# Attention's weight-value products in four visits a pair of heads instead of nine

## The chip, the cores and the metric

The kernel runs on one core of one Trainium2 chip. A core has a matrix engine (TensorE, in the profile PE for matmuls and PEld for the loading of their stationary operand), three engines for elementwise work (VectorE = DVE, ScalarE = ACT, GpSimd = POOL) and a queue that mostly issues DMAs (SyncE = SP). The metric is the device time of one launch in microseconds; lower is better.

## The reference

A decoder trunk with one state-space layer and one attention layer, each followed by a gated convolutional feed-forward block. 1024 tokens and 16 learned meta tokens give 1040 positions of width 1024. The change lies in the attention: 16 heads of width 64, causal without the diagonal, with "stick-breaking" weights in place of a softmax. Cut to what matters:

```python
logits = einsum('bthd,bshd->bhts', q[:, t0:t1], k[:, :t1]) * 64 ** -0.5
visible = s_idx < t_idx
log_keep = where(visible, log_sigmoid(-logits), 0.0)
later = cumsum(log_keep, axis=3, reverse=True) - log_keep
w = exp(where(visible, log_sigmoid(logits) + later, -inf))
out = einsum('bhts,bshd->bthd', w, v[:, :t1])
```

The kernel computes the sum of logarithms as a running product: with keep = sigmoid(-logit) and beta = sigmoid(logit), the weight of key s is beta(s) times the product of keep over all later visible keys.

## The kernel before

The stage before the attention leaves the normalised stream in 16 large SBUF tiles (8 high parts, 8 low parts). The heads are worked off in 8 pairs; the two heads of a pair (index `a`) use the partitions 0 to 63 and 64 to 127. The positions are cut into 9 chunks `i` of 116 (`CB`; the last has 112), and three chunks make a token tile `jj` of 348.

A pair has 18 steps, `steps = [(i, jj) for i in range(9) for jj in range(i // 3, -1, -1)]`: for every chunk of queries the token tiles of keys from its own one back to the first. The loop `for p in range(PAIRS): for n, (i, jj) in enumerate(steps)` does in every step, in this order:

- `weigh(i, jj)`: for either head two matmuls for the logits (L1642, tile `lg`, two PSUM banks), two sigmoids on ScalarE (L1645 `kp` = keep, L1646 `bt` = beta), on the diagonal a mask on GpSimd (L1651), a scan on VectorE for the running product (L1655; a chunk's later tiles begin from the value of the one before) and a multiplication (L1656). `kp` has 6 buffers, `bt` 8.
- `place()`: transposes of projected values (L1606, tile `pv`) and their scaling into `v` on VectorE (L1608).
- half a projection (`half`, matmuls L200 to L202, tile `pj`): 24 matmuls in two steps make a token tile of keys, queries or values; the dictionary `halves` gives each of the 18 steps one half, in steps 0 to 7 for this pair and in 8 to 17 for the next one (keys 0 in steps 8 and 9, queries 0 in 10 and 11, queries 1 in 12 and 13, keys 1 in 14 and 15, values 0 in 16 and 17). `pj` has two PSUM banks, used in turn. A query projection is emptied one step after its second half by `stack` (L1589 on ScalarE, then L1593 on VectorE, tile `qs`), which is put behind that step's scans.
- `chores`: one piece of the preparation of the next pair's weights (L1543 on ScalarE, L1544 on VectorE, tile `wl`).
- `flush(LAG)`: first `values` for a chunk whose weights are complete, then `turn` for the step three before this one.

`turn` transposes the weights of both heads, one block of 116 keys at a time (L1669, tile `wT`, three PSUM banks that `pv` shares), and copies them to SBUF on ScalarE (L1673, tile `wt`). `values` multiplies them with `v` (L1683): for each block `c` of keys two products, one for each head, into the partitions 0 to 63 and 64 to 127 of one PSUM bank `po` (a single buffer); ScalarE copies `po` to `o` (L1684), and at the end of a token tile its queue stores `o` to DRAM (L1686). Those products are in plain float32 and show in the profile as two records each. I call one call of `values` a visit.

`wt` takes its tiles from the pool `Q` of 28 large buffers, in which the stream, the keys, and the queries of token tiles 1 and 2 lie too. SP's queue carries the weight loads and the moves of keys and queries between partitions; the change touches none of them.

In the attention stage PE, DVE, ACT and POOL keep the order of the program (`manual_schedule`); outside of it the scheduler chooses. After the last step, `while turns or ready: flush(0)` empties what is left, and the output projection follows.

Of the kernel before, what the change touches and what calls it, by code (L numbers as in the profile page):

```python
# [10 lines left out]
AF = mybir.ActivationFunctionType  # L11
# [9 lines left out]
CB = 116  # L21
CH = [(c * CB, min(CB, L - c * CB)) for c in range(9)]
TT = [(0, 348), (348, 348), (696, 344)]
TW = 352
QW = 1056
# [37 lines left out]
NPOOL = 3  # L63
DT0 = 0
LAG = 2

NW = 8
SUMS = ((6, 1), (3, 6), (7, 6), (3, 5), (5, 7)), ((4, 7), (2, 1))
# [35 lines left out]
class Trunk:  # L104
# [1085 lines left out]
    def up(self, layer, w0, forms, rest, pool):  # L1190
# [8 lines left out]
        def block(b, t, w, late=None):  # L1199
# [32 lines left out]
            u2 = copy(y)  # L1232
            yield
            z = product(3, (self.ex if next(turn) else self.lg)("p"))
            p5 = copy(z)
            add(z, z, u2)
# [420 lines left out]
            prev[a] = kp  # L1657
        return [bt for _, bt, _ in out]

    def turn(self, i, jj, bt, wt):  # L1660

        nc = self.nc
        nt = CH[i][1]
        blocks = range(3 * jj, min(3 * jj + 3, i + 1))
        for a in range(2):
            pt = self.sm("wT")
            for x, c in enumerate(blocks):
                ns = CH[c][1]
                nc.tensor.transpose(pt[:ns, x * CB : x * CB + nt], bt[a][:nt, x * CB : x * CB + ns], self.ident[:nt, :nt])  # L1669
            spans = [(0, len(blocks), CB)] if CH[blocks[-1]][1] == CB else [(0, 2, CB), (2, 3, CH[8][1])]  # L1670
            for x, y, ns in spans:
                src = pt[:ns, : 3 * CB].rearrange("p (c t) -> p c t", t=CB)[:, x:y, :nt]
                nc.scalar.activation(wt[a][:ns, 3 * jj + x : 3 * jj + y, :nt], src, AF.Copy)  # L1673

    def values(self, p, i, wt, v, o, od):

        nc = self.nc
        t0, nt = CH[i]
        j, c0 = i // 3, (i % 3) * CB
        po = self.ex("po")  # L1680
        for x, c in enumerate(c for jj in range(j, -1, -1) for c in range(3 * jj, min(3 * jj + 3, i + 1))):
            for a in range(2):
                nc.tensor.matmul(po[64 * a : 64 * a + 64, :nt], v[: CH[c][1], c, 64 * a : 64 * a + 64], wt[a][: CH[c][1], c, :nt], start=x == 0, stop=x == i)  # L1683
        nc.scalar.activation(o[:, c0 : c0 + nt], po[:, :nt], AF.Copy)  # L1684
        if i % 3 == 2:
            nc.scalar.dma_start(od[p, :, TT[j][0] : t0 + nt], o[:, : TT[j][1]])  # L1686

    def attention(self, u, pool):


        od = self.dp.tile([PAIRS, P, L], F32, tag="o_d", name="o_d")
        steps = [(i, jj) for i in range(9) for jj in range(i // 3, -1, -1)]

        halves = {(own, n0 + h): (kind, j, h) for own, n0, kind, j in (
            (0, 0, "v", 1), (0, 2, "q", 2), (0, 4, "k", 2), (0, 6, "v", 2),
            (-1, 8, "k", 0), (-1, 10, "q", 0), (-1, 12, "q", 1), (-1, 14, "k", 1), (-1, 16, "v", 0)) for h in range(2)}
        loads = {(-1, 4): "k", (-1, 7): "q", (-1, 9): "v"}
        pairs = [self.heads(u, p, pool) for p in range(PAIRS)]
        turns, ready, wts, os, late, chores = [], [], {}, {}, [], []

        def flush(n):
            while ready:
                p, i = ready.pop()
                if i % 3 == 0:
                    os[p] = self.tmp("o")
                self.values(p, i, wts.pop((p, i)), pairs[p].v, os[p], od)
            if len(turns) > n:
                p, i, jj, bt = turns.pop(0)
                if jj == i // 3:
                    wts[p, i] = [self.Q("wt")[:, : 9 * CB].rearrange("p (c t) -> p c t", t=CB) for _ in range(2)]  # L1710
                self.turn(i, jj, bt, wts[p, i])
                if jj == 0:
                    ready.append((p, i))

        first = pairs[0]
        for kind in "kqv":
            for f in first.load(kind):
                f()
        for kind, j, bank in (("k", 0, self.mm), ("q", 0, self.mm), ("k", 1, self.sm), ("q", 1, self.ex)):
            for h in range(2):  # L1720
                for f in first.half(kind, j, h, bank):
                    f()
            if (kind, j) == ("k", 0):
                self.late_factors()
        self.token_factors(u[KD], pool)
        for p in range(PAIRS):
            prev = None
            for n, (i, jj) in enumerate(steps):
                if jj == i // 3:
                    prev = [None, None]  # L1730
                now = {0: pairs[p], -1: pairs[p + 1]} if p + 1 < PAIRS else {0: pairs[p]}
                bt = self.weigh(i, jj, now[0].qd[i // 3], now[0].ks, prev, pool)
                todo, late = late, []
                now[0].place()
                if p == 0 and n < 2:
                    first.half("v", 0, n)
                for own, pair in now.items():
                    if (own, n) in halves:
                        late += pair.half(*halves[own, n])
                for f in todo + chores[:1]:  # L1740
                    f()
                del chores[:1]
                for own, pair in now.items():
                    if (own, n) in loads:
                        chores += pair.load(loads[own, n])
                flush(LAG)
                turns.append((p, i, jj, bt))
        while turns or ready:
            flush(0)
        return od  # L1750
# [204 lines left out]
```

## Time and profile before

| | |
|---|---|
| Runs before, median of 3 | 2870.42 us (2870.36 to 2876.0) |
| Profiled execution, span from first to last instruction | 2866.2 us; no other time is recorded of it |
| Attention stage | about 1537 to 2065 us of the span |
| PE busy in that stage | 520.9 of 528 us |
| DVE, ACT, POOL busy in it | 451.7, 431.1, 144.7 us |
| Granted TensorE clock in it | 1.00 in every stretch of 60 us up to 2020 us |

Busy time of PE is modelled, since matmuls overlap in the array; a PE that is shown as busy may still stand between two matmuls. In the order of time, a row shows start, duration, engine, line, operation, the tiles written and read, shapes and the number of instructions merged into it; the brackets give the idle time of the engine just before and what ended it.

### The profile page before, as it was taken

The page shows a single profiled execution, that of the slowest core. Times are in us where ns is not written, and L with a number is a line of the kernel's source. Part 1 is how long each engine was busy: PE and PEld are TensorE (multiplying, and loading weights), DVE is VectorE, ACT ScalarE, POOL GpSimd, SP SyncE. Part 2 cuts the span into 40 slices and gives each one's busy share as a digit, 9 for nine tenths or more (in the row PEclk, how much of TensorE's full clock was granted, in tenths as well). Part 3 has the DMA queues.
Part 4 walks back from the last instruction along what each step waited for, and adds up shares of the span by engine and source line. Part 5 has one row for each costly group of instructions (what it writes and reads, how often), then busy time and mean ns, then how long its engine had stood idle before and what let it go on. Part 6 is the DMA issues. An engine that isn't in the chain of part 4 may idle for free.

```text
span 2866.2 us, 58698 instructions
## 1 busy us (share of the span) xinstructions
PE 2824.6 (99%) x21859; PEld 2711.6 (95%) x21859; DVE 2091.2 (73%) x4068; ACT 1631.4 (57%) x3393; POOL 1626.1 (57%) x2440
## 2 busy tenths in 40 slices
PE   8999999999999999999999999999999999999998
PEld 7989999999999999999999999999798999999888
DVE  5676666668597767667887888888759676766776
ACT  5555445543265656565336888887736555555433
POOL 2366464643529888858753222222363888886882
PEclk9999999999999999999999999999999999999999
DMA  4343334333412222244132222222332222225331
GB/s 119 89 114 104 103 91 134 102 132 102 128 60 97 75 82 77 81 162 165 47 128 71 67 62 68 62 58 54 136 118 74 82 78 79 82 81 185 110 103 67
DMA packets 135674, 274.51 MB, mean 96 GB/s; under 512 B 15859, under 2 KB 68220, under 8 KB 135388
## 3 DMA queue, kind: packets, MB, share of 16 engines
q1 hardware_dynamic: 129764, 259.60, 29.1%
q0 software_dynamic: 2048, 6.49, 0.6%
q10 hardware_dynamic: 3576, 4.67, 0.5%
q8 instruction: 172, 2.82, 0.4%
q14 instruction: 114, 0.93, 0.1%
HBM read 204.63 MB, written 51.16 MB: 89 GB/s over the span
## 4 chain that ended last, share of the span: by engine, by line
PE 91%; DVE 4%; ACT 2%; POOL 1%; issue 1%; DMA 0%; DVEq 0%; ACTq 0%; SPq 0%; POOLq 0%
PE p L200 10%; PE p L202 10%; PE p L201 10%; PE acc L200 8%; PE acc L201 8%; PE acc L202 8%; PE pj L200 8%; PE pj L201 8%; PE pj L202 8%; PE po L1683 3%; PE lg L1642 2%; PE wT L1669 2%; PE y L801 1%; PE S L790 1%; PE y L803 1%
## 5 line engine op out<-in xcount | busy, mean ns | idle before, releaser
L100 POOL TENSOR_TENSOR wl<-w,wh 128x256 fp32r<-128x256 f32 x768 | 686.1, 924 | 365.0 <-ACT wh L187 265.4
L200 PE MATMUL pj<-uh,wh 128*128 128x348 f32 (+2 forms) x1536 | 500.8, 327 | 2.2 <-DVE xbc L330 1.4
L201 PE MATMUL pj<-ul,wh 128*128 128x348 f32 (+2 forms) x1536 | 494.8, 322 | 0.8 <-DVE ul L311 0.8
L202 PE MATMUL pj<-uh,wl 128*128 128x348 f32 (+2 forms) x1536 | 491.9, 320 | 0.0
L200 PE MATMUL p<-bh,fh 128*128 128x262 f32 (+1 forms) x1408 | 401.0, 285 | 5.7 <-DVE p L1226 5.5
L202 PE MATMUL p<-bh,fl 128*128 128x262 f32 (+1 forms) x1408 | 401.0, 285 | 1.9 <-POOL fl L100 1.9
L201 PE MATMUL p<-bl,fh 128*128 128x262 f32 (+1 forms) x1408 | 398.2, 283 | 0.0
L100 POOL TENSOR_TENSOR fl<-x,fh 128x256 fp32r<-128x256 f32 x352 | 265.0, 786 | 190.3 <-ACT fh L1163 164.4
L201 PE MATMUL p<-bl,wh 128*128 128x262 f32 (+1 forms) x1040 | 295.4, 284 | 1.3 <-DVE bl L1087 1.3
L200 PE MATMUL p<-bh,wh 128*128 128x262 f32 (+1 forms) x1040 | 295.4, 284 | 0.0
L200 PEld LDWEIGHTS pj<-uh,wh 128*128 128x128 f32 x1536 | 288.7, 188 | 5.6 <-ACT xbc L327 1.7
L202 PE MATMUL p<-bh,wl 128*128 128x262 f32 (+1 forms) x1040 | 293.9, 283 | 0.0
L201 PEld LDWEIGHTS pj<-ul,wh 128*128 128x128 f32 x1536 | 289.2, 188 | 2.4 <-DVE ul L311 1.4
L202 PEld LDWEIGHTS pj<-uh,wl 128*128 128x128 f32 x1536 | 288.7, 188 | 0.1
L330 DVE SCALAR_TENSOR_TENSOR c<-p,params,c 128x260 f32<-128x260 f32 (+1 forms) x528 | 248.5, 480 | 54.8 <-ACT c L327 48.3
L200 PEld LDWEIGHTS p<-bh,fh 128*128 128x128 f32 x1408 | 267.8, 190 | 6.7 <-DVE p L1226 5.9
L202 PEld LDWEIGHTS p<-bh,fl 128*128 128x128 f32 x1408 | 266.6, 189 | 2.8 <-POOL fl L100 2.5
L201 PEld LDWEIGHTS p<-bl,fh 128*128 128x128 f32 x1408 | 267.8, 190 | 0.1
L1223 ACT ACTIVATE ft<-p 128x262 f32<-128x262 f32 (+1 forms) x352 | 133.4, 382 | 178.3 <-DVE p L1226 110.3
L201 PE MATMUL acc<-gl,wh 128*128 128x260 f32 (+1 forms) x672 | 214.2, 320 | 0.0
L202 PE MATMUL acc<-gh,wl 128*128 128x260 f32 (+1 forms) x672 | 213.3, 319 | 0.0
L200 PE MATMUL acc<-gh,wh 128*128 128x260 f32 (+1 forms) x672 | 210.8, 320 | 0.1
(344 smaller groups left out, 7918.7 us busy)
## 6 DMA issues: line engine op xcount, KB each, us to landing
w<-in_w_up SPq DMA_DIRECT2D x88, 512.0 KB
w<-in_w_down SPq DMA_DIRECT2D x44, 512.0 KB
w<-in_w_in SPq DMA_DIRECT2D x40, 512.0 KB
E<-ea_d SPq DMA_DIRECT2D x32, 464.0 KB
D<-acs_d SPq DMA_DIRECT2D x32, 420.5 KB
g<-c SPq DMA_DIRECT2D x88, 130.0 KB
g<-c SPq DMA_DIRECT2D x88, 128.0 KB
b<-g SPq DMA_DIRECT2D x16, 520.0 KB
```

Of the source, the lines that this page charges most:

```text
L100: done.append(eng.tensor_tensor(out[:, c], x[:, c], y[:, c], op=op))
L200: self.behind(mm(out, wh, uh, start=first, stop=False, skip_group_check=joins), tie, "behind the sums of squares")
L201: mm(out, wh, ul, start=False, stop=False, skip_group_check=joins)
L202: self.last_mm = mm(out, wl, uh, start=False, stop=last, skip_group_check=joins)
L330: ins = nc.vector.scalar_tensor_tensor(out, ps[:, o + i : o + i + n], wcol(i), out, op0=ALU.mult, op1=ALU.add)
L790: nc.tensor.matmul(ps, bk[:n], xde[:n].rearrange("p h d -> p (h d)"), start=True, stop=True)
L801: nc.tensor.matmul(y, xdt[:n, i, :], dk[:, i, :], start=True, stop=c == 0)
L803: nc.tensor.matmul(y, state[:, i, :], ce[:, i, :], start=False, stop=True)
L1223: nc.scalar.activation(s[:, :N], ps[:, :N], AF.Copy)
L1642: nc.tensor.matmul(ps[:nt, :m], part[:, c0 : c0 + nt], ks[a][:, s0 : s0 + m], start=x == 0, stop=x == 1)
L1669: nc.tensor.transpose(pt[:ns, x * CB : x * CB + nt], bt[a][:nt, x * CB : x * CB + ns], self.ident[:nt, :nt])
L1683: nc.tensor.matmul(po[64 * a : 64 * a + 64, :nt], v[: CH[c][1], c, 64 * a : 64 * a + 64], wt[a][: CH[c][1], c, :nt], start=x == 0, stop=x ...
```

## The change

`values` is called for four groups of chunks a pair of heads rather than for each of the nine: chunks 0 to 2, 3 to 5, 6 and 7, and 8. The weights of a group's chunks lie side by side in `wt`, so that for a block of keys one product covers all chunks of the group that see it: in group (3, 4, 5) blocks 0 to 3 have 348 columns, block 4 has 232 and block 5 has 116. A group is visited in the step after the last `turn` of its last chunk. The tiles `wt` hold three blocks of keys for groups of three, four for (6, 7) and nine for (8), and a group has as many tiles as it needs. The copies from `wT` are cut where a tile ends.

```diff
+VISITS = (0, 1, 2), (3, 4, 5), (6, 7), (8,)
...
+    def weight_tiles(self, visit):
+        width = len(visit) * CB
+        each = min(QW // width, visit[-1] + 1)
+        return [[self.Q("wt")[:, : each * width].rearrange("p (c t) -> p c t", t=width) for _ in range(0, visit[-1] + 1, each)] for _ in range(2)]
...
-            spans = [(0, len(blocks), CB)] if CH[blocks[-1]][1] == CB else [(0, 2, CB), (2, 3, CH[8][1])]
-            for x, y, ns in spans:
+            cuts = {0, len(blocks)} | {x for x, c in enumerate(blocks) if c % each == 0 or CH[c][1] != CB}
+            cuts = sorted(cuts)
+            for x, y in zip(cuts, cuts[1:]):
+                ns, (q, c) = CH[blocks[x]][1], divmod(blocks[x], each)
                 src = pt[:ns, : 3 * CB].rearrange("p (c t) -> p c t", t=CB)[:, x:y, :nt]
-                nc.scalar.activation(wt[a][:ns, 3 * jj + x : 3 * jj + y, :nt], src, AF.Copy)
+                nc.scalar.activation(wt[a][q][:ns, c : c + y - x, t0 : t0 + nt], src, AF.Copy)
...
-    def values(self, p, i, wt, v, o, od):
+    def values(self, p, visit, wt, v, o, od):
+        first, last = visit[0], visit[-1]
+        j, c0 = first // 3, first % 3 * CB
+        end = CH[last][0] + CH[last][1]
+        n = end - CH[first][0]
+        each = wt[0][0].shape[1]
         po = self.ex("po")
-        for x, c in enumerate(c for jj in range(j, -1, -1) for c in range(3 * jj, min(3 * jj + 3, i + 1))):
+        order = [*range(first, last + 1), *range(first - 1, -1, -1)]
+        for x, c in enumerate(order):
+            t0 = max(c - first, 0) * CB
+            q, r = divmod(c, each)
             for a in range(2):
-                nc.tensor.matmul(po[64 * a : 64 * a + 64, :nt], v[: CH[c][1], c, 64 * a : 64 * a + 64], wt[a][: CH[c][1], c, :nt], start=x == 0, stop=x == i)
-        nc.scalar.activation(o[:, c0 : c0 + nt], po[:, :nt], AF.Copy)
-        if i % 3 == 2:
-            nc.scalar.dma_start(od[p, :, TT[j][0] : t0 + nt], o[:, : TT[j][1]])
+                nc.tensor.matmul(po[64 * a : 64 * a + 64, t0:n], v[: CH[c][1], c, 64 * a : 64 * a + 64], wt[a][q][: CH[c][1], r, t0:n],
+                                 start=x == 0, stop=x == last, skip_group_check=True)
+        nc.scalar.activation(o[:, c0 : c0 + n], po[:, :n], AF.Copy)
+        if last % 3 == 2:
+            nc.scalar.dma_start(od[p, :, TT[j][0] : end], o[:, : TT[j][1]])
...
-                self.turn(i, jj, bt, wts[p, i])
-                if jj == 0:
-                    ready.append((p, i))
+                visit = next(v for v in VISITS if i in v)
+                if (p, visit) not in wts:
+                    wts[p, visit] = self.weight_tiles(visit)
+                self.turn(i, jj, bt, wts[p, visit], visit[0])
+                if jj == 0 and i == visit[-1]:
+                    ready.append((p, visit))
```

More of the change, by code (lines that the diff above doesn't have):

```diff
@@ L1658, in weigh, with turn @@
         return [bt for _, bt, _ in out]
-    def turn(self, i, jj, bt, wt):
+    def weight_tiles(self, visit):
+        width = len(visit) * CB
+        each = min(QW // width, visit[-1] + 1)
+        return [[self.Q("wt")[:, : each * width].rearrange("p (c t) -> p c t", t=width) for _ in range(0, visit[-1] + 1, each)] for _ in range(2)]
+    def turn(self, i, jj, bt, wt, first):
         nc = self.nc
         nt = CH[i][1]
+        t0 = (i - first) * CB
+        each = wt[0][0].shape[1]
         blocks = range(3 * jj, min(3 * jj + 3, i + 1))
@@ L1669, in turn @@
                 nc.tensor.transpose(pt[:ns, x * CB : x * CB + nt], bt[a][:nt, x * CB : x * CB + ns], self.ident[:nt, :nt])
-            spans = [(0, len(blocks), CB)] if CH[blocks[-1]][1] == CB else [(0, 2, CB), (2, 3, CH[8][1])]
-            for x, y, ns in spans:
+            cuts = {0, len(blocks)} | {x for x, c in enumerate(blocks) if c % each == 0 or CH[c][1] != CB}
+            cuts = sorted(cuts)
+            for x, y in zip(cuts, cuts[1:]):
+                ns, (q, c) = CH[blocks[x]][1], divmod(blocks[x], each)
                 src = pt[:ns, : 3 * CB].rearrange("p (c t) -> p c t", t=CB)[:, x:y, :nt]
-                nc.scalar.activation(wt[a][:ns, 3 * jj + x : 3 * jj + y, :nt], src, AF.Copy)
-    def values(self, p, i, wt, v, o, od):
+                nc.scalar.activation(wt[a][q][:ns, c : c + y - x, t0 : t0 + nt], src, AF.Copy)
+    def values(self, p, visit, wt, v, o, od):
         nc = self.nc
-        t0, nt = CH[i]
-        j, c0 = i // 3, (i % 3) * CB
+        first, last = visit[0], visit[-1]
+        j, c0 = first // 3, first % 3 * CB
+        end = CH[last][0] + CH[last][1]
+        n = end - CH[first][0]
+        each = wt[0][0].shape[1]
         po = self.ex("po")
-        for x, c in enumerate(c for jj in range(j, -1, -1) for c in range(3 * jj, min(3 * jj + 3, i + 1))):
+        order = [*range(first, last + 1), *range(first - 1, -1, -1)]
+        for x, c in enumerate(order):
+            t0 = max(c - first, 0) * CB
+            q, r = divmod(c, each)
             for a in range(2):
-                nc.tensor.matmul(po[64 * a : 64 * a + 64, :nt], v[: CH[c][1], c, 64 * a : 64 * a + 64], wt[a][: CH[c][1], c, :nt], start=x == 0, stop=x == i)
-        nc.scalar.activation(o[:, c0 : c0 + nt], po[:, :nt], AF.Copy)
-        if i % 3 == 2:
-            nc.scalar.dma_start(od[p, :, TT[j][0] : t0 + nt], o[:, : TT[j][1]])
+                nc.tensor.matmul(po[64 * a : 64 * a + 64, t0:n], v[: CH[c][1], c, 64 * a : 64 * a + 64], wt[a][q][: CH[c][1], r, t0:n],
[3 more added lines that the diff above has]
+            nc.scalar.dma_start(od[p, :, TT[j][0] : end], o[:, : TT[j][1]])
     def attention(self, u, pool):
@@ L1702, in flush @@
             while ready:
-                p, i = ready.pop()
-                if i % 3 == 0:
+                p, visit = ready.pop()
+                if visit[0] % 3 == 0:
                     os[p] = self.tmp("o")
-                self.values(p, i, wts.pop((p, i)), pairs[p].v, os[p], od)
+                self.values(p, visit, wts.pop((p, visit)), pairs[p].v, os[p], od)
             if len(turns) > n:
                 p, i, jj, bt = turns.pop(0)
-                if jj == i // 3:
-                    wts[p, i] = [self.Q("wt")[:, : 9 * CB].rearrange("p (c t) -> p c t", t=CB) for _ in range(2)]
-                self.turn(i, jj, bt, wts[p, i])
-                if jj == 0:
-                    ready.append((p, i))
+                visit = next(v for v in VISITS if i in v)
[4 more added lines that the diff above has]
+                    ready.append((p, visit))
         first = pairs[0]
```

## The prediction

> **What bounds the kernel now.** I read the page first, then the waits of the attention stage (1537 to 1998 us: the eight head pairs without the tail), then one pair after another by windows, and last the order of time around the places where TensorE waited.
>
> ```profile
> span 2866.2 us, 58698 instructions
> PE 2824.6 (99%) x21859; PEld 2711.6 (95%) x21859; DVE 2091.2 (73%) x4068; ACT 1631.4 (57%) x3393; POOL 1626.1 (57%) x2440
> PE 91%; DVE 4%; ACT 2%; POOL 1%; issue 1%; DMA 0%; DVEq 0%; ACTq 0%; SPq 0%; POOLq 0%
> ```
>
> By the page TensorE (PE) is the bound everywhere: 99% busy, 91% of the chain. Anything taken off TensorE should then come off the time. The waits of the attention stage, and two stretches of pair 3 and of pair 4, say something else:
>
> ```profile
> ACT o L1684 <- PE po L1683: 45.9, 26, 3.0
> DVE kp L1655 <- ACT kp L1645: 16.5, 7, 2.6
> PEld po L1683 <- issue: 9.9, 46, 0.2
> PEld pj L200 <- DVE qs L1593: 0.8, 3, 0.4
> ...
> 1734.49:1752.19 17.70, 17.70 (x171) 16.83 (x170) 12.28 (x24) 10.85 (x35) 7.08 (x26) 1.00 0.08 22
> 1752.19:1794.30 42.11, 42.11 (x358) 39.24 (x357) 39.18 (x80) 38.24 (x110) 9.56 (x44) 1.00 0.29 77
> 1794.30:1818.20 23.90, 23.51 (x212) 22.56 (x211) 17.83 (x32) 15.52 (x46) 7.28 (x28) 1.00 0.13 31
> 1818.20:1860.58 42.38, 42.38 (x360) 39.61 (x359) 39.15 (x80) 38.61 (x111) 9.43 (x44) 1.00 0.29 79
> ```
>
> In the windows the columns after the length are busy times of PE, PEld, DVE, ACT and POOL. I number a pair's 18 calls of weigh as steps 0 to 17. The cut points are the first scan of step 4 (1752.19, 1818.20) and the end of the second copy of the next pair's queries in step 14 (1794.30, 1860.58). Between them VectorE has 39.18 us of work in 42.11, and nearly all of the rest is the 0.10 to 0.13 us that it stands still between a scan and the multiplication that reads it:
>
> ```profile
> L1655 DVE TENSOR_TENSOR_SCAN kp<-kp,kp,one 116x349 f32<-116x349 f32 x14 | 13.2, 944 | 2.4 <-ACT kp L1645 2.4
> L1656 DVE TENSOR_TENSOR bt<-bt,kp 116x348 f32<-116x348 f32 (+2 forms) x22 | 10.6, 482 | 2.7
> ```
>
> The 2.7 us are those pauses, and 39.2 + 2.7 = 41.9 of 42.1. So from step 4 to step 14 VectorE works in one unbroken chain, whatever TensorE does in the meantime; only in steps 0 to 3, where the tiles are short, does it wait. TensorE is tied to that chain twice in a pair:
>
> ```profile
> 1752.19 0.94 DVE L1655 TENSOR_TENSOR_SCAN kp<-kp,kp,one 116x349 f32<-116x349 f32 x1 [2.42 <-ACT kp L1645]
> 1785.92 1.06 DVE L1593 TENSOR_TENSOR qs<-pj,qs 64x348 fp32r<-64x348 f32 x2
> 1787.04 0.19 PEld L200 LDWEIGHTS pj<-uh,wh 128*128 128x128 f32 x1 [0.17 <-DVE qs L1593]
> 1792.25 1.61 PE L1683 MATMUL po<-wt,v 116*64 116x116 f32 x28
> 1793.23 1.07 DVE L1593 TENSOR_TENSOR qs<-pj,qs 64x348 fp32r<-64x348 f32 x2
> 1793.79 0.61 PE L1669 MATMUL wT<-ident,bt 116*116 116x116 f32 x4
> 1794.17 0.87 PE L1642 MATMUL lg<-k,qs 128*112 128x348 f32 x4
> 1794.72 0.19 PEld L200 LDWEIGHTS pj<-uh,wh 128*128 128x128 f32 x1
> ```
>
> The projections have two PSUM banks. In step 14 the projection of the next pair's keys needs the bank that the first query copy (1785.92 to 1786.98) empties: its weights load at 1787.04, 0.06 later, after a wait. In step 16 the projection of values needs the bank that the second copy empties (1794.30): it loads at 1794.72, with only 1794.72 - 1794.30 - 0.06 = 0.36 us in hand. Earlier than this TensorE cannot get there.
>
> **The change, part by part.**
>
> *Column work: none saved.* With the causal cut a chunk's products still cover the same blocks: a pair has 1+2+...+9 = 45 blocks of about 116 columns for either head, before and after. Products fall from 90 to 52 a pair (two records each), but the time goes by columns:
>
> ```profile
> 1778.47 0.32 PE L202 MATMUL pj<-uh,wl 128*128 128x348 f32 x1
> 1778.63 0.76 PE L1669 MATMUL wT<-ident,bt 116*116 116x116 f32 x6
> ...
> 1774.32 1.21 PE L1683 MATMUL po<-wt,v 116*64 116x116 f32 x20
> ...
> 1781.40 0.32 PE L202 MATMUL pj<-uh,wl 128*128 128x348 f32 x1
> 1781.65 1.41 PE L1683 MATMUL po<-wt,v 116*64 116x116 f32 x24
> 1782.99 0.41 PE L1669 MATMUL wT<-ident,bt 116*116 116x116 f32 x2
> ...
> 1737.16 1.81 PE L1683 MATMUL po<-wt,v 116*64 116x116 f32 x32
> ...
> 271.53 0.74 PE L665 MATMUL ms<-z,ones 128*128 128x348 f32 x2
> L665 PE MATMUL ms<-z,ones x6: 452/454/458, 271.5 to 284.3; 128*128 128x348 f32 x4, 128*128 128x344 f32 x2
> ```
>
> Twelve more records (1.81 against 1.21) are six passes of both heads: 0.60/6 = 0.10 us a pass of 116 columns. Transposes of 116 columns take (0.76 - 0.26)/5 = 0.10 each alone, so the two heads do run side by side. A pass of 348 columns takes 0.74 - 0.45 = 0.29, three times 0.10 less 0.01. A pass thus costs 0.82 to 0.86 ns a column and at most 7 ns for itself; 304 passes fewer are worth 0 to 2.1 us in the whole kernel, and I take 0.5.
>
> *Visits: nine become four a pair, 40 fewer in all.* From the last projection matmul to the first transpose it is 1782.99 - 1781.40 = 1.59 us with a visit of twelve passes and 0.16 without one: 1.59 - 1.20 - 0.16 = 0.23 for getting in and out. The first transpose after it is slow too: four records in 0.61 after a visit, six in 0.76 without, 0.05 more than two records fewer explain. That is 0.28 a visit, 11.2 us for 40. This is the change's gain, if TensorE can use it.
>
> The Trainium skill has this as a rule: "TensorEngine Tiling (Array Packing)", Key Properties, says that changing the tiling mode (not just the tile) drains TensorE. The trace agrees, with 0.28 us for the way in and out.
>
> *Where the products go.* Now: those of chunks 0, 1, 2 in steps 4, 5, 6; 3, 4, 5 in steps 8, 10, 12; 6 in step 15; 7 in step 0 of the next pair; 8 in its step 3. After: (0-2) in step 6, (3-5) in step 12, (6, 7) in step 0 of the next pair, (8) in its step 3. Followed around the cycle of a pair:
>
> - Steps 4 to 13: the same columns and four visits fewer, TensorE is 4 x 0.28 = 1.1 us early at step 14. There it already waits for the first query copy, which VectorE's chain puts at the same place. Worth 0: the wait grows from 0.17 to about 1.2 us, or part of it shows earlier, at the bank that the values' transposes share with wT in steps 9 and 10.
> - Step 15: the product of chunk 6 leaves, 14 passes x 0.10 + 0.28 = 1.7 us. TensorE comes to the projection of step 16 that much earlier and can use the 0.36, and some 0.05 because a load that waited lies under its own first matmul: 0.41. The other 1.3 us become a wait for the second query copy.
> - Step 0: the visit of chunk 7 (16 passes of 116 columns) becomes that of 6 and 7: 16 passes again, 14 of 232 columns and two of 116. It is 14 x 116 = 1624 columns more, at 0.82 to 0.86 ns 1.33 to 1.40 us; I take 1.36. Nothing covers it: the row 1794.30 to 1818.20 has 23.51 of PE in 23.90, and the first scan of step 4 waits at its end for exactly this chain (2.42 us behind ScalarE's kp, which waits for lg). No row has a 232-column pass of this shape; the bounds are the two prices by column.
> - Step 3: (8) is as before.
>
> So a pair's cycle, one VectorE chain and one TensorE stretch, changes by +1.36 - 0.41 = +0.95 us. It is closed seven times: 6.65, less what the fewer passes and a little more slack in pair 0 give, 6.5 us.
>
> *ScalarE.*
>
> ```profile
> L1684 ACT ACTIVATE o<-po x72: 242/268/484, 1556.0 to 2062.7; 128x116 f32<-128x116 f32 x64, 128x112 f32<-128x112 f32 x8
> L1673 ACT ACTIVATE wt<-wT x304: 257/451/752, 1551.8 to 2060.8; 116x348 f32<-116x348 f32 x72, 116x116 f32<-116x116 f32 x24, 116x232 f32<-116x232 f32 x24, 116x224 f32<-116x224 f32 x16
> ```
>
> Copies of po fall from 72 to 32 wider ones, 40 x 0.27 = 10.8 us less busy time and some 2 to 4 back for the width; copies of wT rise by 32 (chunks 6 and 7 have tiles of four blocks, so that blocks 3 to 5 are cut after the first), 32 x 0.26 = 8.3 more. Both lie in an engine with 38.24 in 42.11 that is ahead of VectorE. I take 0; without that cover it is 0 to 1 us. Its copy of po now waits behind longer visits (45.9 us in 26 waits now), queued in front of the copies of wT and the next sigmoids. These need matmuls that come after the visit anyway, so 0 again.
>
> *DMA, buffers, tail.* The 24 stores of o go out at the ends of chunks 2, 5 and 8 as now: 0. A visit (3-5) or (6, 7) holds four large tiles in place of two; with the 16 of the stream, keys and queries this fills the 28 buffers in steps 6 to 8. Those reused belong to products that TensorE has already run when the transposes write: 0. In pair 7 nothing projects and VectorE sets the end:
>
> ```profile
> 2058.76 0.48 PE L1669 MATMUL wT<-ident,bt 112*116 112x112 f32 x3 [1.04 <-DVE bt L1656]
> 2060.27 0.47 PE L1669 MATMUL wT<-ident,bt 112*116 112x112 f32 x3 [1.03 <-DVE bt L1656]
> ```
>
> The 1.4 us more of the last visit (6, 7) fall ahead of these 2.07 us of waits: 0, bounds -1 and +1.
>
> The sum is made on the profiled execution: span 2866.2, after it 2872.7. The median of the runs, 2870.4, lies 4.2 above the span; I carry that over: 2876.9, +0.23%. Bounds of the unknown: 7 x (1.30 - 0.45) - 1 - 2 = 3 to 7 x (1.40 - 0.36) + 1 + 1 = 9.3 us, thus 2873.4 to 2879.7.
>
> **The rivals.**
>
> *Faster: the visits' overhead comes off whole.* If VectorE's chain does not hold step 16, pairs 0 to 6 lose 35 x 0.28 = 9.8 us, with the passes 10 to 12: 2860. It decides against me once the slack at step 16 is over 1.36 us rather than 0.36. For it: PE 99%, and 9.9 us of "issue" before po. Against: 41.9 of 42.1 us on VectorE, and the wait at step 14 that stands there already. Chance 0.12. By the rule of the drain alone (the Trainium skill, "TensorEngine Tiling (Array Packing)", Key Properties) this would be the result.
>
> *No change.* VectorE's chain shrinks by some 0.5 us or more of 42 a pair, because TensorE reads the same memories at other times (scan and multiplication differ by up to 0.1 us now): 7 x (0.95 - 0.5) = 3 us, 2873, or less. Nothing shows that it would. Chance 0.13.
>
> *Much slower.* Passes of 232 and 348 columns do not run side by side: visit (6, 7) costs another 2.9 us, 7 x 2.9 + 6.5 = 27, thus 2897; or VectorE starts its chain late behind a longer wait of ScalarE, 0.5 us a pair, 2880.5. The 0.05 us a record speaks against the first. Chance 0.05 together.
>
> **How the numbers follow.** My forecast has 0.70. No change can be told within 0.2%, 5.7 us, thus below 2876.1; the sum lies just above, so of the 0.70 some 0.47 are slower and 0.23 the same. Slower 0.47 + 0.05, same 0.23 + 0.13, faster 0.12. The range 2867 to 2880.5 takes in the forecast's bounds, the no-change case and the mild slower one, and leaves out the faster case and the serial passes; the forecast's own range is 2873.4 to 2879.7.
>
> **What would show it.** After the change: 32 copies of po, 832 records of po and 336 copies of wT; the step from the last projection to the first transpose at 0.23 above its passes still; a pair's cycle up from about 66.0 to 67 us; the stretch from the end of the second query copy to the first scan of step 4 up from 23.9 to about 24.9, and the one of VectorE's chain still at 42.1 to 42.4; "pj L200 <- DVE qs" up from 0.8 us to 10 or more, twice a pair, at steps 14 and 16. The forecast is wrong if that chain comes out well below 42, if there is no wait at step 16, or if (6, 7) costs other than 2.9 to 3.0 us.

## The result and the profile after

The changed kernel takes 2879.22 us (median of 6 runs, 2879.05 to 2881.42) against 2870.48 us (6 runs, 2870.17 to 2876.0): a ratio of 1.003, 95% interval 1.0019 to 1.004. It is slower, by 8.7 us. The forecast was 2876.9 in a range of 2867 to 2880.5.

The head of the page and the chain of work that ended last, after the change:

```profile
span 2877.3 us, 57495 instructions
PE 2819.9 (98%) x21251; PEld 2692.5 (94%) x21251; DVE 2091.9 (73%) x4068; ACT 1627.3 (57%) x3385; POOL 1624.0 (56%) x2440
PE 85%; DVE 6%; ACT 5%; issue 1%; POOL 1%; DMA 1%; ACTq 0%; DVEq 0%; SPq 0%; POOLq 0%
```

PE is busy 4.7 us less and the span is 11.1 us longer, so TensorE stands more. By the share of busy time (98%) one would not see it; the chain does, where PE falls from 91% to 85% and VectorE and ScalarE together rise from 6% to 11%. The seven closed cycles of a pair account for it: each is 1.60 us longer, 11.2 together. The waits of the attention stage, 1537 to 2010 us, and the four stretches of pairs 3 and 4 that were shown of before (columns as there):

```profile
ACT o L1704 <- PE po L1702: 49.8, 19, 3.5
DVE kp L1656 <- POOL kp L1652: 23.1, 15, 2.8
ACT k L1577 <- DVE k L1566: 22.0, 14, 2.6
DVE kp L1656 <- ACT kp L1646: 16.9, 7, 2.7
...
PEld lg L1643 <- ACT bt L1647: 10.6, 20, 0.6
PE wT L1679 <- DVE v L1609: 7.0, 8, 1.0
...
PE lg L1643 <- ACT bt L1647: 5.9, 14, 0.5
...
PEld pj L201 <- DVE qs L1594: 4.6, 7, 1.0
PEld po L1702 <- issue: 4.1, 19, 0.2
...
1738.00:1757.61 19.61, 19.14 (x170) 17.43 (x169) 12.39 (x25) 11.47 (x36) 7.75 (x27) 1.00 0.07 20
1757.61:1799.76 42.15, 40.45 (x285) 36.65 (x283) 39.23 (x80) 38.63 (x110) 8.98 (x44) 1.00 0.27 77
1799.76:1825.16 25.40, 24.88 (x208) 23.07 (x209) 17.81 (x33) 15.09 (x47) 7.29 (x28) 1.00 0.13 33
1825.16:1867.31 42.15, 40.46 (x285) 36.65 (x283) 39.23 (x80) 38.64 (x110) 9.00 (x44) 1.00 0.28 77
```

VectorE's chain from the first scan of step 4 to the second query copy is 42.15 us as before; the stretch behind it is 25.40 in place of 23.90. Three waits of TensorE that hardly stood in the list of before are new: for VectorE's scaling of values (`v`), for ScalarE's sigmoids (`bt`), and for the query copies (`qs`). The row to look at is the third: ScalarE stands 22.0 us for VectorE's `k`. Before, in the window 1537 to 1998 us, the rows of `k`, `v` and `bt` were:

```profile
ACT k L1576 <- DVE k L1565: 8.9, 8, 1.5
...
PE wT L1669 <- DVE v L1608: 0.9, 1, 0.9
...
PE lg L1642 <- ACT bt L1646: 0.4, 1, 0.4
```

In the order of time, around step 16 of pair 3 and step 0 of pair 4 of the changed kernel:

```profile
1798.69 1.07 DVE L1594 TENSOR_TENSOR qs<-pj,qs 64x348 fp32r<-64x348 f32 x2
...
1799.81 0.43 PE L201 MATMUL pj<-uh,wh 128*128 128x348 f32 x1 [0.30 <-DVE qs L1594]
...
1801.84 0.76 PE L1679 MATMUL wT<-ident,bt 116*116 116x116 f32 x6
...
1802.73 0.52 DVE L1566 TENSOR_TENSOR k<-pj,r 128x348 f32<-128x348 f32 x1
...
1803.29 0.50 ACT L1577 ACTIVATE k<-k 128x348 fp32r<-128x348 f32 x1 [2.17 <-DVE k L1566]
1803.69 0.92 ACT L1685 ACTIVATE wt<-wT 116x116 f32<-116x116 f32 x4
...
1804.47 0.58 ACT L1646 ACTIVATE kp<-lg,rt 112x348 f32<-112x348 f32 x1
...
1805.54 0.41 PE L1643 MATMUL lg<-k,qs 128*116 128x116 f32 x2
...
1805.77 0.60 ACT L1647 ACTIVATE bt<-lg,rt 112x348 f32<-112x348 f32 x1
...
1806.42 0.41 PE L1643 MATMUL lg<-k,qs 128*116 128x116 f32 x2 [0.47 <-ACT bt L1647]
...
1808.48 0.32 PE L203 MATMUL pj<-uh,wl 128*128 128x348 f32 x1
1808.73 3.16 PE L1702 MATMUL po<-wt,v 116*64 116x232 f32 x32
...
1811.82 0.79 PE L1679 MATMUL wT<-ident,bt 112*116 112x112 f32 x6
```

The second query copy ends at 1799.76 and the projection of step 16 starts 0.05 later: TensorE is held there, as forecast. Then ScalarE's copy of the next pair's keys (`k`, L1577, the first thing that `key` issues in step 16) stands 2.17 us for VectorE's product of step 15 (L1566), which waits its turn in the chain until 1802.73. Behind that copy on ScalarE stand the copies of `wT` and the sigmoids. They come late, the bank of `lg` is emptied late, and TensorE stands 0.47 us at the second head's logits of step 0. Last, visit (6, 7), 32 records in 3.16 us where chunk 7 alone had 32 in 1.81.

The Trainium skill, "PSUM — Partial Sum Buffer", Engine vs sequencer instructions, says that the queues of ScalarE, VectorE and GpSimd are strict first in, first out. The trace agrees: ScalarE stands 2.17 us ahead of the key copy and first copies `wT` at 1803.69, though those transposes are done at 1802.60 (1801.84 + 0.76).

The kernel before had the same wait of ScalarE at this place, shorter, and in pair 3 the same wait of TensorE behind it:

```profile
1798.17 0.50 ACT L1576 ACTIVATE k<-k 128x348 fp32r<-128x348 f32 x1 [1.54 <-DVE k L1565]
...
1801.19 0.41 PE L1642 MATMUL lg<-k,qs 128*116 128x116 f32 x2 [0.39 <-ACT bt L1646]
```

In the other six of its pairs 0 to 6 TensorE stands at most 0.06 us there; after the change it is 0.47 us in every one.

To place the difference I took, for each of the pairs 0 to 6, the start of the first matmul of `lg` in step 4 as zero, and then the mean over the seven pairs of the times at which things begin in that cycle (us; "wT in 10" is the first transpose of weights in step 10, "pj in 14" and "pj in 16" the first projection matmul of steps 14 and 16; "q end" is the end of the second query copy; "lg 0" is the second head's logits in step 0 of the next pair, "step 1" the first logits of its step 1; the last column is the next step 4 and thus the cycle):

| kernel | wT in 10 | pj in 14 | q end | pj in 16 | lg 0 | step 1 | cycle |
|---|---|---|---|---|---|---|---|
| before | 24.82 | 36.44 | 43.67 | 44.26 | 50.26 | 54.85 | 66.01 |
| after | 23.42 | 37.32 | 43.84 | 43.90 | 50.50 | 56.45 | 67.61 |

From row to row: up to step 16 -0.36, from there to "lg 0" 6.60 against 6.00, +0.60, from there to step 1 5.95 against 4.59, +1.36, and from step 1 to step 4 11.16 both times. The sum is +1.60. The first and third of these stood in the prediction as -0.41 and +1.36; the second did not stand there. The cycles are those of one profiled execution of each kernel; the stretches of the span outside the seven cycles differ by some 8 us between the kernels below, mostly where their work is the same, so that the medians of the runs follow the cycles only to a few us.

### The profile page after: what moved, and what is told of

Its sections match the earlier page's. It is cut to its first block, busy times and chain, and to the rows that moved or that the text cites. A ratio compares the mean times of both kernels' runs of the same rounds, so it can differ in the third digit from the quotient of the medians.

```text
span 2877.3 us, 57495 instructions
## 1 busy us (share of the span) xinstructions
PE 2819.9 (98%) x21251; PEld 2692.5 (94%) x21251; DVE 2091.9 (73%) x4068; ACT 1627.3 (57%) x3385; POOL 1624.0 (56%) x2440
## 4 chain that ended last, share of the span: by engine, by line
PE 85%; DVE 6%; ACT 5%; issue 1%; POOL 1%; DMA 1%; ACTq 0%; DVEq 0%; SPq 0%; POOLq 0%
PE p L203 10%; PE p L201 10%; PE p L202 10%; PE acc L201 8%; PE acc L203 8%; PE acc L202 8%; PE pj L201 7%; PE pj L202 7%; PE pj L203 7%; PE po L1702 2%; PE lg L1643 2%; ACT bt L1647 1%; PE wT L1679 1%; ACT kp L1646 1%; PE y L802 1%
```

## The experiments

Theory V was that VectorE's chain, and ScalarE's key copy behind it, hold TensorE, so that the saved ways in and out of visits don't come off. Its rivals were that the visits themselves cost more than by columns (long visits, sets of tiles, wide passes). All kernels are given with the ratio to the kernel before on the same chip and its 95% interval.

**Parts of the change.** Three of the first four are the changed kernel with other groups:

```diff
-VISITS = (0, 1, 2), (3, 4, 5), (6, 7), (8,)
+VISITS = (0,), (1,), (2,), (3,), (4,), (5,), (6, 7), (8,)      # e1: only 6 and 7 together
+VISITS = (0, 1, 2), (3, 4, 5), (6,), (7,), (8,)                # e2: 6 and 7 apart
+VISITS = (0,), (1,), (2,), (3,), (4,), (5,), (6,), (7, 8)      # e4: 7 and 8 together, its tiles taken when first written
```

and e3 has the four groups of the change, with each product cut into pieces of 116 columns:

```diff
+            for b in range(t0, n, CB):
+                e = min(b + CB, n)
                 for a in range(2):
-                    nc.tensor.matmul(po[64 * a : 64 * a + 64, t0:n], ...
+                    nc.tensor.matmul(po[64 * a : 64 * a + 64, b:e], ...
```

(In e3 every piece of the first block carries `start`, and the sums come out wrong; number, shape and order of the products are as said.)

> Only the chunks 6 and 7 share a visit; the chunks 0 to 5 have one each again. Theory V (VectorE's chain from step 4 to step 14 and ScalarE's key copy behind it hold TensorE at step 16 and at step 0, so that the product of chunk 6, moved from step 15 to step 0, is no longer covered): the cycle of a pair stays at 67.5 us as with all four groups, since where TensorE stands before step 14 plays no part; 2878 to 2880 us. Rival L (long visits cost by themselves, the engine being held for 3 us at a time): two of the three long visits are gone, so the loss of 8.7 us shrinks to about 4, 2874 to 2875 us. Rival T (the larger sets of weight tiles cost): likewise about 2875 us.

Measured: 2882.47 us, ratio 1.0038 (1.0024 to 1.0051), cycle 67.49. This one group, which saves one visit of nine, carries nearly the whole loss. Its cycle divides like that of the change: step 16 at 43.78 (-0.48), to "lg 0" 6.60, to step 1 5.95. V holds in the cycle; the median of the runs lies 2.5 us above what V gave, and the profiled execution, the fastest of the five, has 2879.57.

> Chunks 0 to 2 and 3 to 5 share visits, the chunks 6, 7 and 8 have one each. Theory V: chunk 6's product is back in step 15, so step 0 has no more work than before. The trace of the changed kernel shows TensorE reaching step 14 about 0.9 us late (37.3 us after step 4 rather than 36.4), because the products of chunks 3 and 4 left steps 8 and 10, where it then waited, and came back in step 12; this stays: 7 x 0.9 = 6 us, about 2876 us, and no wait for the query copy at steps 14 and 16. If only the moved product of chunk 6 counted, 2870 us. Rival L: one long visit less of three, 2874 to 2876 us; this run alone does not tell it from V, the one with only 6 and 7 together does.

Measured: 2873.91 us, ratio 1.0008 (0.9999 to 1.0017), cycle 66.46: +0.45 where V had +0.9. TensorE does come late, to step 14 at 37.23 (+0.79) and to step 16 at 44.97 (+0.71), though two groups of three save four visits ahead of it. But 0.2 of that comes back at "lg 0", where it now waits less for ScalarE than before (5.79 us from step 16, 6.00 before). So four visits fewer made a pair 0.45 us longer in the profiled execution, and the mechanism was right but not its size; in the runs the interval still takes in 1. Most of where TensorE was held is in the waits:

```profile
ACT k L1577 <- DVE k L1566: 12.9, 15, 3.8
...
PE wT L1679 <- DVE v L1609: 6.9, 8, 1.0
...
PE lg L1643 <- ACT bt L1647: 2.9, 8, 0.4
```

0.9 us a pair (6.9 in 8 waits) is the wait of step 10's transposes for a PSUM bank that VectorE's scaling of values has to empty first. Another 0.4 a pair is a late ScalarE again.

> The four groups and their places stay, but every product is cut into pieces of one chunk's columns (116), so that there are as many products as with nine visits. Theory V: what counts is where the work lies; 304 passes more at 2 to 7 ns are 0.6 to 2 us: 2880 to 2881 us. Rival W (passes of 232 and 348 columns are dear in themselves, for instance because the two heads no longer run side by side): back to 2870 us or below.

Measured: 2879.48 us, ratio 1.003 (1.0018 to 1.0041), cycle 67.63. The answer of the trace on its products:

```profile
L1704 PE MATMUL po<-wt,v x1440: 257/263/314, 1562.7 to 2075.6; 116*64 116x116 f32 x144, 116*64 116x112 f32 x32, 112*64 112x112 f32 x4
```

All 1440 records of before are back and the cycle is the same within 0.02 us. The time goes by columns; wide passes neither gain nor lose here.

> Nine visits become eight: the chunks 7 and 8 share one, at the place of chunk 8 (step 3), so that chunk 7's product leaves step 0. Both places lie in the stretch from step 16 to step 4, which TensorE alone sets. Theory V: one way in and out of 0.28 us saved in each of 7 cycles, 2 us: 2868 to 2869 us. Rival L: the visit is 3.3 us long, longer than any of the changed kernel, so 2873 us or more.

Measured: 2872.07 us, ratio 1.0 (0.9991 to 1.0009), cycle 65.80. One visit fewer, in steps 0 to 3 where TensorE is not held, takes 0.21 us off the cycle of the profiled execution (0.28 expected). In the runs the expected 2868 to 2869 wasn't reached: seven times 0.21 is 1.5 us, and the trace shows more than that lost at the end of pair 7, where the last visit now holds both chunks and takes 6.08 us (36 records) in place of 1.95.

**What holds TensorE.** V had been formed on the trace of after; the next experiments move work in the queues and change no work. With "keys late" the next pair's key copies come one step later:

```diff
-                todo, late = late, []
+                todo, late, later = late, later, []
...
-                        late += pair.half(*halves[own, n])
+                        kind, todo_next = halves[own, n][0], pair.half(*halves[own, n])
+                        if own and kind == "k":
+                            later += todo_next
+                        else:
+                            late += todo_next
```

> The changed kernel, but the next pair's key copies on ScalarE (and what follows them) are issued one step later, at steps 11 and 17 in place of 10 and 16. Work is the same. Theory V (in the changed kernel ScalarE's key copy waits for VectorE's k<-pj,r, the copies of wT and the sigmoids queue behind it, and TensorE then waits for the banks of lg; this is the 0.65 us a pair that the prediction missed): the waits 'ACT k <- DVE k' fall from 22.0 us to under 6 and those of lg on ACT bt from 16.5 us to under 5; the cycle of a pair falls from 67.6 to 67.0-67.2 us, 2875 to 2877 us. It does not go below 67.0, since step 16 is still held by the second query copy. Rival (the late ScalarE only covers a wait that TensorE has anyway, or the longer visits themselves cost more than by columns): the cycle stays at 67.5-67.7 us, 2879 us.

Measured: 2874.52 us, ratio 1.0015 (1.0006 to 1.0024), cycle 66.75.

```profile
PEld pj L201 <- DVE qs L1594: 8.9, 8, 1.3
PE wT L1679 <- DVE v L1609: 7.0, 8, 1.0
PE pj L201 <- DVE qs L1594: 6.4, 7, 1.0
...
ACT k L1577 <- DVE k L1566: 3.8, 1, 3.8
...
PEld lg L1643 <- ACT bt L1647: 2.3, 6, 0.4
```

0.86 us a pair and 4.7 us in the runs come from the place of the key copies in the queues alone (VectorE's subtraction and three DMA moves, which follow ScalarE's copy, come a step later with it). ScalarE's wait is gone, and that of TensorE for the logits nearly; instead TensorE comes early to step 16 and stands there 0.9 us (6.4 / 7), the wait that the prediction had put at 1.3. I had said that the cycle would not go below 67.0; it does, because the kernel before has 0.2 of ScalarE's wait itself, which goes too (f3 below has 5.78 us from step 16 to "lg 0" in place of 6.00).

To tell which of the two key copies matters, this moves only the second (`if own and n == 15`):

> The changed kernel, but only the second of the next pair's two key copies comes a step later (step 17 in place of 16); the first stays at step 10. Theory V (a wait ahead of step 16 is swallowed there, since TensorE must stand until the second query copy is done; one behind it adds to the cycle): the wait at step 12 stays (some 0.6 us), TensorE still comes late to step 14 (37.3 us after step 4 begins) and to step 16 at 43.8 to 43.9 us, and from there to the second lg of the next pair's step 0 it takes 5.9 us in place of 6.6: cycle 66.8 to 66.9 us, 2875 us, as with both moved (66.75). Rival (either key copy costs its own wait, 0.4 to 0.5 us a pair): cycle 67.1 to 67.3 us, 2877 us.

Measured: 2874.21 us, ratio 1.0017 (1.0008 to 1.0026), cycle 66.76, the same as with both. TensorE waits at step 12 as before (step 14's projection starts at 37.26), and step 16 swallows it (43.82). Here a wait counts only behind the last place that holds anyway.

**All three places.** In addition to keys late: the next pair's query copies, and the values' transposes, ahead of the step's `weigh`.

```diff
+                for f in early:
+                    f()
+                early = []
+                now[0].place()
                 bt = self.weigh(i, jj, now[0].qd[i // 3], now[0].ks, prev, pool)
-                todo, late = late, []
-                now[0].place()
+                todo, late, later = late, later, []
...
+                        elif own and kind == "q":
+                            early += todo_next
```

> The changed kernel with three reorderings and no other work: the next pair's query copies (ScalarE and VectorE) are issued ahead of the step's weigh instead of behind it, the values' transposes (pv) too, and the key copies one step later. Theory V (TensorE is held by VectorE's chain only because the query copies, the values' multiplication and the key copies stand late in the queues): the second query copy ends some 2.9 us earlier against the chain, step 16 is held no longer, and the saved ways in and out of visits come through: 35 x 0.28 = 9.8 us below before, cycle 64.6 to 65.2 us, 2860 to 2866 us. Rival (the visits with chunks side by side cost TensorE more by themselves, wherever VectorE stands): no better than keys late alone, cycle 67.0 or more, 2875 us or more.

Measured: 2861.06 us, ratio 0.9967 (0.9955 to 0.998), cycle 65.03. This beats both kernels, by 10.0 us the one before. By the profiled executions 7 x 0.98 = 6.9 us of it lie in the seven cycles and 1.1 between the first logits of pair 0 and its step 4 (14.12 us in place of 15.22); the rest isn't placed.

> The kernel before with the same three reorderings. Theory V: TensorE hardly waits for VectorE there (0.17 us at step 14, 0.36 us in hand at step 16), so that little is to be had: cycle 65.5 to 65.9 us, 2867 to 2870 us. Rival (the reorderings are good by themselves, whatever the visits): as much off as from the changed kernel, 2858 to 2863 us.

Measured, on the kernel before: 2870.95 us, ratio 1.0 (0.9991 to 1.0008), cycle 65.78. By themselves the moves bring the cycle only the 0.23 us of ScalarE's wait at "lg 0", and the runs nothing. So it is the visits saved that the moves let through: 65.78 - 65.03 = 0.75 us a pair. Two more kernels leave out one of the three:

> The changed kernel with key copies one step later and query copies ahead of weigh, but the values' transposes behind weigh as in the changed kernel. Theory V (three places of VectorE's chain hold TensorE in the changed kernel, each for itself: the values' multiplication at step 10, the second query copy at step 16, the key copies by way of ScalarE): step 16 is held no longer, but step 10 still is (1.0 us, with keys late at 23.4 us after step 4 begins), from there 42.8 us to the next step 4 as with all three moves: cycle 66.1 to 66.3 us, 2867 to 2871 us, between keys late alone (66.75) and all three moves (65.03). Rival (the query copies alone hold TensorE, the bank at step 10 only shows a wait that it would have elsewhere): cycle 65.0 to 65.2, 2861 us.

Measured, query copies early, values' transposes late: 2871.41 us, ratio 0.9996 (0.9986 to 1.0005), cycle 65.78. It lies below what V gave (66.1 to 66.3) and above the rival (65.0 to 65.2): step 10 holds TensorE for 0.75 us of the cycle (65.78 against 65.03), not for the 1.1 to 1.3 that V's cycle took.

> The changed kernel with key copies one step later and the values' transposes ahead of weigh, but the query copies behind weigh as in the changed kernel. Theory V (the second query copy at the end of VectorE's chain holds step 16, whatever TensorE gained before): the wait at step 10 goes and comes back at step 14 and step 16, cycle 66.6 to 66.8 us as with keys late alone (66.75), 2873 to 2876 us; 'pj <- DVE qs' grows from about 15 to over 20 us. Rival (the bank of step 10 is what holds, the query copies hardly do): cycle 65.6 or less, 2866 us or less.

Measured, the other way round: 2875.74 us, ratio 1.001 (1.0001 to 1.0019), cycle 66.79, as V said. Freed at step 10, TensorE stands for the query copies instead:

```profile
PEld pj L201 <- DVE qs L1594: 14.2, 14, 1.3
PE pj L201 <- DVE qs L1594: 10.0, 14, 1.0
```

In one table, with the columns of above:

| kernel | wT in 10 | pj in 14 | q end | pj in 16 | lg 0 | step 1 | cycle |
|---|---|---|---|---|---|---|---|
| keys late | 23.34 | 36.64 | 43.74 | 43.79 | 49.69 | 55.59 | 66.75 |
| and place early | 22.28 | 36.52 | 43.77 | 43.83 | 49.71 | 55.93 | 66.79 |
| and queries early | 23.37 | 36.64 | 40.74 | 42.93 | 48.72 | 54.62 | 65.78 |
| all three | 22.31 | 35.89 | 40.71 | 42.17 | 47.95 | 54.17 | 65.03 |
| before, all three | 24.85 | 36.42 | 40.71 | 44.27 | 50.05 | 54.92 | 65.78 |

Rows one and two: the 1.06 us won at step 10 are lost again by step 14 and 16, where the start stays 0.05 to 0.06 behind "q end". Only when "q end" has gone ahead by 3 us does it count.

**Two misses.** Both try to lighten the chain or its waits. With the low parts of the weights (24 instructions a pair of VectorE) made on GpSimd:

```diff
-                return [lambda: some(0), lambda: some(KD // 2)] if p else [scale, parts]
+                return [scale, parts]
```

> The changed kernel with the low parts of pairs 1 to 7's weights (wl, 24 instructions of 0.29 us a pair on VectorE) made on GpSimd as for pair 0 already (scaled there, one rounding copy on ScalarE, subtracted there). Theory V: VectorE's chain from step 4 to step 14 falls from 42.1 to about 35 us, TensorE is held nowhere, and the saved ways in and out of visits come through: cycle 64.6 to 65.2 us, 2860 to 2866 us. Against it: GpSimd gets 24 pieces of 0.8 to 0.9 us a pair in front of its masks (affine_select), which can put single scans 2 to 3 us late; TensorE is two steps behind, so I expect none of it to show. Rival (the visits themselves cost more): cycle 67.0 or more, 2875 us or more.

Measured: 2892.73 us, ratio 1.0076 (1.0063 to 1.0088), cycle 69.49. The weights come too late for the projection of step 10, in the order of time of one pair:

```profile
1783.11 1.06 ACT L1534 ACTIVATE wh<-w 128x1024 fp32r<-128x1024 f32 x1 [2.43 <-POOL kp L1640]
...
1784.22 0.43 PE L201 MATMUL pj<-uh,wh 128*128 128x348 f32 x1 [1.07 <-ACT wh L1534]
...
1785.98 0.66 PE L203 MATMUL pj<-uh,wl 128*128 128x348 f32 x1 [1.18 <-POOL wl L101]
```

TensorE stands 2.25 us in this one step. VectorE waits longer for GpSimd's masks too:

```profile
DVE kp L1656 <- POOL kp L1652: 39.9, 29, 2.8
```

That is 39.9 us against 23.1 after the change, and from the first scan of step 4 to "q end" it is 44.12 us, not the 35 that I had expected. The chain was not shortened, so this says nothing of V.

With all three moves, and keys' and queries' weights loaded a step earlier (`{(-1, 3): "k", (-1, 6): "q", (-1, 9): "v"}`):

> The changed kernel with all three reorderings (query copies and values' transposes ahead of weigh, key copies one step later), and the next pair's key and query weights loaded and split one step earlier (loads at steps 3 and 6 in place of 4 and 7). With the three reorderings TensorE still waits 1.6 us in all for wl at step 11. Theory V (that wait is one of those that TensorE's fewer visits have uncovered): it goes, 0.2 us a pair, cycle 64.8 to 64.9 us, 2859 to 2860 us. Against it: VectorE's work of step 4 to 14 only changes place, so the wait could come back at another (65.0, 2861 us).

Measured: 2867.47 us, ratio 0.9985 (0.9976 to 0.9995), cycle 65.66. The wait for `wl` is gone, but the cycle is 0.63 longer than without this: TensorE now waits longer for ScalarE's sigmoids, presumably because ScalarE's part of the weights stands in front of those of other steps; no run takes this apart.

```profile
PEld lg L1643 <- ACT bt L1647: 8.2, 22, 0.5
```

With the three moves alone it was 4.2 us in 13 waits.

## Why the prediction was right, and where not

- *What is run.* As forecast, by the lines of the changed kernel's products and copies:

```profile
L1704 ACT ACTIVATE o<-po x32: 264/406/527, 1563.5 to 2074.9; 128x348 f32<-128x348 f32 x16, 128x232 f32<-128x232 f32 x8, 128x112 f32<-128x112 f32 x8
...
L1702 PE MATMUL po<-wt,v x832: 257/359/508, 1561.8 to 2074.6; 116*64 116x232 f32 x58, 116*64 116x112 f32 x51, 116*64 116x348 f32 x32, 116*64 116x116 f32 x20
...
L1685 ACT ACTIVATE wt<-wT x336: 247/398/758, 1552.3 to 2073.0; 116x116 f32<-116x116 f32 x56, 116x348 f32<-116x348 f32 x56, 116x232 f32<-116x232 f32 x24, 116x224 f32<-116x224 f32 x16
```

- *What bounds the kernel.* Right. VectorE's chain stayed at 42.15 us, and the projection of step 16 starts 0.06 us behind its end (43.90 against 43.84).
- *Steps 4 to 13: early, but worth 0.* The worth was right, the way was not. The gain goes at the alternative of the sentence, the bank of the values' transposes in step 10 (7.0 us in 8 waits), and with a wait at step 12, which wasn't named, TensorE even comes 0.9 late to step 14. There, "the wait grows to about 1.2 us" was wrong; "pj <- DVE qs" is 4.6 us once a pair, not 10 or more twice. The lateness costs nothing only because step 16 holds anyway (h1); in e2, where step 16 does not hold, the pair is 0.45 us longer.
- *Step 15: -0.41.* Measured -0.36.
- *Step 0: +1.36, uncovered.* Measured +1.36; the visit of 232 columns lies at the price by column, and e3 confirms that price. The row of 3.16 us, less the 0.21 by which chunk 7's row exceeded its 16 passes (1.81 - 1.60), is 2.95, inside the 2.9 to 3.0 that the forecast stood on.
- *Visits, 0.28 us a way in and out.* No run measures it by itself. Around visit (6, 7) the trace has 1811.82 - 1808.48 = 3.34 us from the last projection matmul to the first transpose; less 0.16 and passes of 2.85 to 2.99 this is 0.19 to 0.33, which takes in the 0.23. In the cycles, e4 has 0.21 for one visit, and f2 against f3 0.75 for five, where 0.28 each would give 1.40. By step 10's transposes 18 passes of 0.10 and four visits, 2.92 us, should be gone, and 2.54 are (24.85 - 22.31): 0.38 of the missing 0.65 is lost by then. f2 still has these waits of TensorE's weight loads, the second of them at step 11:

```profile
PEld lg L1643 <- ACT bt L1647: 4.2, 13, 0.4
...
PEld pj L203 <- DVE wl L1545: 1.6, 6, 0.3
```

  They were not taken away singly, so their shares of the 0.65 stay open.
- *ScalarE: "I take 0".* This is the step that failed. The term was bounded at 0 to 1 us in all, and the stretch from step 16 to "lg 0" is 0.60 us a pair longer, 4.2 in seven. 0.48 of it is ScalarE's lateness: with the keys late the stretch falls by 0.70 after the change (f1, 6.60 to 5.90), and with the three moves by 0.22 in the kernel before (f3, 6.00 to 5.78). The other 0.11 is TensorE's held start at step 16: without ScalarE's wait the stretch is 5.90 where step 16 holds (f1) and 5.79 where it doesn't (e2). I had summed its work (38 of 42 us) and called it ahead of VectorE; but it issues in order, and twice a pair the thing at its head waits for VectorE itself. The row "ACT k <- DVE k: 8.9, 8, 1.5" was in the trace of before, and so was the wait of 0.39 us at the second head's logits, 1801.19. The change made the wait of TensorE longer because TensorE starts step 16 0.06 us behind "q end" in place of 0.59, while ScalarE's copies keep to VectorE's chain: what is gained at step 16 turns into a wait behind it. ScalarE also has two more copies of `wT` there (four in 0.92 us at 1803.69, where the kernel before had two in 0.80); no run takes their part in the 0.48 apart. The mild form of the third rival, "a longer wait of ScalarE, 0.5 us a pair, 2880.5", had the size, with another place: the first scan of step 4, where nothing changed (11.16 us from step 1 both times).
- *With that wait off on both sides,* the cycle of f1 is 66.75 and that of f3 65.78: +0.97, where the prediction had +0.95.
- *The median.* Per pair I was 0.65 low, 4.6 us in seven. The carried 4.2 us between the span and the median were 2.3 too many: 2879.22 - 2877.3 = 1.9 after the change. The profiled execution of before lay some 2.3 us below the median of its runs, and the 4.2 held that too. Together: 2876.9 + 4.6 - 2.3 = 2879.2. That 2879.2 lies inside the forecast's own 2873.4 to 2879.7 is thus luck: the two errors went against each other, and between the profiled executions the difference is 11.1 us, above the forecast's bound of 9.3.
- *The rival that ends faster, 2860,* is what f2 reached with 2861.06, in part by luck: its 9.8 us were all to come from 35 visits, and f2 has 7 x 0.75 = 5.3 from them. Its condition was over 1.36 us in hand at step 16 of the kernel before. With the moves, that kernel starts step 16 3.56 us behind "q end" (f3, 44.27 - 40.71) in place of 0.59, and f2 still has 1.46 (42.17 - 40.71), so that step 16 holds no longer. That is needed but not enough: g1 has 2.19 (42.93 - 40.74) and its cycle gains nothing over f3, for step 10 holds.

The Trainium skill's rule of the drain ("TensorEngine Tiling (Array Packing)", Key Properties) speaks for fewer changes of mode. The cycles agree in the sign where TensorE is free (e4, f2 against f3), and the change itself shows that the rule says nothing about whether an engine elsewhere holds the saved time.

## What to carry over

Before counting what a busier engine saves, list the places at which it takes a buffer from another engine, and when that buffer can come free at the earliest. In this kernel, time saved ahead of the last such place turned into a wait, and work moved behind it counted in full; and an in-order engine with 8% of idle time is no cover when the head of its queue waits for the engine that sets the pace. Here, moving three short pieces within the queues turned a change that cost 8.7 us into one that saves 10.0 (6.9 of them in the cycles of the pairs), while the runs of the same moves without the change saved nothing.

## What was not expected of the hardware

A matmul that starts after a stand takes longer: the first one of step 16, at 1799.81, has 0.43 us where the next have 0.32. Cutting the products in two and three pieces, 608 records more in the whole kernel, cost 0.02 us a pair. GpSimd, free for 33 of 42 us, could not take over 7 us of VectorE's work (f4): it delivered the weights late, and VectorE's chain grew to 44.12 us instead of shrinking.
